# A blocked log-sum-exp over heads: three heads instead of two on TensorE and ScalarE in the half units of tiles 60 and 61

## The chip, the cores and the metric

The kernel runs on one core of one Trainium2 chip. A time is the device time of one execution in microseconds (us). The time before is the median of three executions. A profile is one further execution, taken with the hardware profiler on.

The engines are TensorE (PE; its weight loads are shown as PEld), VectorE (DVE), ScalarE (ACT), GpSimd (POOL) and SyncE (SP), which issues the transfers.

## What is computed

`x` is 8 x 2048 x 2048 (batch, row, column) in fp32, `bias` is 8 x 256. A row of x is cut into 8 heads of 256 columns. For each row and head the result is the log-sum-exp of 256 biased values, written twice next to each other:

```python
x_heads = x.reshape(B, S, H, Dh).transpose(0, 2, 1, 3)
x_heads = x_heads + bias[None, :, None, :]
x_tiled = np.repeat(x_heads, 2, axis=2)
mx = x_tiled.max(axis=-1, keepdims=True)
lse = mx.squeeze(-1) + np.log(np.exp(x_tiled - mx).sum(axis=-1))
```

The kernel sums exponentials without subtracting the maximum, and at its end judges from the largest and smallest sum whether that was safe. If it was not, everything is computed again in a careful way; with these inputs it isn't.

## The kernel before

**Tiles.** 64 tiles of 256 rows each are worked through in order: 128 partitions, with K = 2 rows to a partition. The input lies in four buffers `xb` of four rows each, so that eight tiles are on the chip at a time. When tile t is done, the load of tile t + 8 is put on SP's queue (`reload`); from tile 42 on tiles are loaded one by one, and from tile 57 on in pieces of one row (a half unit).

**Ways to a sum of exponentials.** For one head of one row there are four:
- TensorE writes the bias into a PSUM bank (`put_bias`: a bf16 product of ones with the bias in three parts, L320) and adds x to it by a product with the identity (`add_x`, L338: two passes, since the data are fp32). ScalarE then takes the exponential from PSUM and sums it in the same instruction (`sum_biased`, L393, with a second small instruction that reads the sum).
- ScalarE takes the exponential of x without the bias (`exp_inplace`, L418), and VectorE multiplies it by exp(bias) and sums (`weigh`, L453, one instruction a head and a small one that reads the sum). The factors exp(bias) lie in `one_ps` for heads 1 and 2, `w_ps` for heads 3 to 6 and `w_sb` for 6 and 7.
- The same exponential, but GpSimd multiplies and folds the 256 columns to 32 by halving (`fold`, L469 and L477), and VectorE sums the 32 (`add_fold`, L483).
- In the bulk, GpSimd adds the bias beforehand (L412), and VectorE sums seven heads with one instruction (L437).

**Stages.** A table `STAGES` says from which tile on which mode holds. A mode gives `pe`, the number of heads that TensorE biases; `acc`, those that ScalarE sums; `g0`, from which head on GpSimd adds the bias (8: none); and `fold`, how many heads GpSimd folds. Tiles 0 to 53 are `BULK`, 54 to 56 `MIXED`. From tile 57 on each row of a tile has its own mode: `PROMPT_F1` (two heads on TensorE and ScalarE, five weighed, one folded) in 57 to 61, `SINGLE_F1` (one, six, one) in 62, and in 63 first `PROMPT_F2` (two, four, two) and then `TRIPLE` (three, five, none).

**Order.** The order on each engine is that in which the program issues instructions; it is written out by hand, and the framework adds the waits. A half unit of tiles 57 to 62 issues:
1. `add_x` for this unit's heads on TensorE;
2. `put_bias` for the next unit, then `keep_warm`: three products of the identity with itself into a spare bank, for nothing but activity;
3. what the units before left for later in `for_pool`: VectorE's sum of a folded head, and reloads;
4. `exp_inplace` on ScalarE for all heads that TensorE doesn't have, in one instruction; `fold` on GpSimd;
5. what the unit before left in `for_pe`: its `sum_biased` on ScalarE;
6. `weigh` on VectorE.

The unit's own `sum_biased` is then put into `for_pe`. So on ScalarE the sums of a unit come behind the exponential of the next one.

**PSUM.** Four banks of 512 columns (`ps`, in two tiles called `pair`) take the biased heads of these units in turn. A row with two heads fills one bank. A row with three heads takes one bank for heads 0 and 1 and another, with 256 columns, for head 2.

**End.** After the last sum TensorE transposes the sums of the last batch, ScalarE takes the logarithm, SP stores it; VectorE and TensorE form the verdict, and all engines branch on it.

Of the kernel before, what the change touches and what calls it, by code (L numbers as in the profile page):

```python
# [34 lines left out]
MIXED = dict(pe=1, acc=1, g0=4, late=False, fold=0)  # L35
PROMPT_F1 = dict(pe=2, acc=2, g0=8, late=False, fold=1)
PROMPT_F2 = dict(pe=2, acc=2, g0=8, late=False, fold=2)
SINGLE_F1 = dict(pe=1, acc=1, g0=8, late=False, fold=1)
TRIPLE = dict(pe=3, acc=3, g0=8, late=False, fold=0)
FOLD = 32  # L40
# [8 lines left out]
    (0, (BULK,)),  # L49
    (54, (MIXED,)),  # L50
    (57, (PROMPT_F1, PROMPT_F1)),
    (62, (SINGLE_F1, SINGLE_F1)),
    (63, (PROMPT_F2, TRIPLE)),
]
# [8 lines left out]
def kernel(  # L63
# [9 lines left out]
    H, Dh = bias.shape  # L73
# [8 lines left out]
    MM = 512  # L82
# [42 lines left out]
    def modes_of(t):  # L125
        return [modes for t0, modes in STAGES if t0 <= t][-1]

    def pieces(t):

        if len(modes_of(t)) == 1:  # L130
            return [(0, K, 0, D)]
        cols = [[(0, D)]] * K if t < T - 1 else LAST_COLS
        return [(k, k + 1, c0, c1) for k in range(K) for c0, c1 in cols[k]]
# [59 lines left out]
    def reload(t):  # L193

        n = t + NBUF
        if n < BLOCKS:
            if n % TB == TB - 1:
                load(n - TB + 1)
        elif n < T:
            load(n)  # L200
# [65 lines left out]
    def first_factors():  # L266
        spread(one_ps, V0, W0)
        nc.scalar.activation(out=one_ps, in_=one_ps, func=ACT.Exp)

    def other_factors():  # L270
        nc.scalar.activation(
            out=w_ps[:, W_LATE - W0 :], in_=b_rep[:, W_LATE - G0 : W2 - G0], func=ACT.Exp
        )
        nc.scalar.activation(out=w_sb, in_=b_rep[:, W1 - G0 :], func=ACT.Exp)
# [56 lines left out]
    def add_x(m, t, k0, c0, c1, got):  # L331


        heads = []
        for ka, kb, c, w, bank, p in got:
            if not c0 <= c < c1:
                continue
            mm = nc.tensor.matmul(  # L338
                p,
                lhsT=ident,  # L340
                rhs=xts[t % NBUF][:, ka:kb, c : c + w],
                start=False,
                stop=True,
            )
            on_bank(bank, on_x(t, mm, [loads[t, k0, c0]]))
            for i in range(0, (kb - ka) * w, Dh):
                k, cw = divmod(i, w)
                heads.append((ka + k, (c + cw) // Dh, bank, p[:, i : i + Dh], mm))
        return heads

    def keep_warm():
        for _ in range(NWARM):
            nc.tensor.matmul(  # L353
                tp[:, 0], lhsT=ident, rhs=ident, start=True, stop=True
            )

    def late_heads(m, t, got, sums):


        mms = []  # L360
        for h, p in enumerate(got[:-1]):
            mm = nc.tensor.matmul(  # L362
                p,
                lhsT=ident,
                rhs=xts[t % NBUF][:, :, h * Dh : (h + 1) * Dh],
                start=False,
                stop=True,
            )
            mms.append(on_x(t, mm, [loads[t, 0, 0]]))

        def pe_part():
            for k in range(K):
                act = nc.scalar.activation(  # L373
                    out=xts[t % NBUF][:, k, 0:Dh],
                    in_=got[0][:, k * Dh : (k + 1) * Dh],
                    func=ACT.Exp,
                    accum_out=sums[:, k, 0:1],
                )
                last_uses[t].append(on_x(t, act, [mms[0]]))
            act = nc.scalar.activation(  # L380
                out=xts[t % NBUF][:, :, Dh : m["pe"] * Dh].rearrange(
                    "p k (h j) -> p h k j", j=Dh
                ),
                in_=got[-1].rearrange("p (h k j) -> p h k j", k=K, j=Dh),
                func=ACT.Exp,
            )
            on_x(t, act, [mms[-1]])

        return pe_part

    def sum_biased(t, k, h, bank, p, mm, sums):

        act = nc.scalar.activation(  # L393
            out=xts[t % NBUF][:, k, h * Dh : (h + 1) * Dh],
            in_=p,
            func=ACT.Exp,
            accum_out=sums[:, k, h : h + 1],
        )
        last_uses[t].append(on_bank(bank, on_x(t, act, [mm])))
# [9 lines left out]
    def g_add(m, t, k0, k1):  # L409
        c = m["g0"] * Dh  # L410
        v = xts[t % NBUF][:, k0:k1, c:D]
        add = nc.gpsimd.tensor_tensor(  # L412
            out=v, in0=v, in1=each_row(b_rep, c - G0, D - c, k1 - k0), op=ALU.add
        )
        return on_x(t, add, [loads[t, k0, 0]])

    def exp_inplace(t, v, after):
        return on_x(t, nc.scalar.activation(out=v, in_=v, func=ACT.Exp), [after])  # L418
# [90 lines left out]
    def store():  # L509

        nc.sync.dma_start(
            out=out[0 : B - 1].rearrange("b h (n r) -> (h n) b r", n=NB),
            in_=res.rearrange("q b p k r -> q b (p k r)"),
        )
# [104 lines left out]
    def sums_of(t):  # L619

        b, blk = divmod(t, NBLK)
        if b < B - 1:
            return R[b][:, blk % TB * K :, :, blk // TB]
        return R_last[:, :, blk, :].rearrange("p h k -> p k h")
# [4 lines left out]
    for_pe = []  # L629
# [10 lines left out]
    def flush(later_work):  # L640
        for f in later_work:
            f()
        later_work.clear()

    for t in range(T):
        if t == T_FACTORS:
            other_factors()
        xt = xts[t % NBUF]
        sums = sums_of(t)
        for k0, k1, c0, c1 in pieces(t):  # L650
            m = modes_of(t)[k0]
            add = None
            heads = []
            if c0 == 0:
                bias_here = bias_there
            if m["late"]:
                pe_part = late_heads(m, t, bias_here, sums)
            else:
                heads = add_x(m, t, k0, c0, c1, bias_here)

                def pe_part(t=t, heads=heads, sums=sums):
                    for k, h, bank, p, mm in heads:
                        sum_biased(t, k, h, bank, p, mm, sums)

            if c0 == 0:
                if next_units and not m["late"]:
                    bias_there = put_bias(*next_units.pop(0))
                if t > T_PROMPT and m["g0"] == H:
                    keep_warm()
                if m["g0"] < H:  # L670
                    add = g_add(m, t, k0, k1)
                if t < T - 1 or k0 == 0:
                    flush(for_pool)
            if t == T_PROMPT and (k0, c0) == (0, 0):
                first_factors()
            h0 = max(c0 // Dh, m["pe"])
            h1 = min(c1 // Dh, m["g0"])
            hf = max(h0, min(h1, H - m["fold"]))
            if h0 < h1 and not m["late"]:
                done = exp_inplace(  # L680
                    t, xt[:, k0:k1, h0 * Dh : h1 * Dh], loads[t, k0, c0]
                )
                if hf < h1:
                    for_pool.append(fold(t, k0, hf, h1, sums, done))
            if c0 == 0:
                flush(for_pe)
            if not m["late"]:
                for k in range(k0, k1):
                    for h in range(h0, hf):
                        weigh(  # L690
                            t,
                            xt[:, k, h * Dh : (h + 1) * Dh],
                            h,
                            sums[:, k, h : h + 1],
                            done,
                        )

            def pool_part(t=t, m=m, k0=k0, k1=k1, sums=sums, add=add):
                if add:
                    later(m, t, k0, k1, sums, add)  # L700
                if k1 == K:
                    reload(t)

            for_pool.append(pool_part)
            if m["g0"] < H:
                pe_part()
                if m["late"]:
                    bias_there = put_bias(*next_units.pop(0))
            elif heads:
                for_pe.append(pe_part)  # L710

        fb, at = divmod(t - 2, NBLK)
        if fb >= 0 and at == NBLK - 1:
            finish(fb)
            ends_of(fb)
            if fb == B - 2:
                store()
# [39 lines left out]
```

## Time and profile before

| | |
|---|---|
| median of 3 executions | 326.43 us (326.16 to 326.53) |
| the profiled execution | 327.41 us |
| its span, first to last instruction | 325.5 us |
| mean granted TensorE clock | 0.909 |
| PE busy | 272.7 us (84%) |
| DVE busy | 289.4 us (89%) |
| ACT busy | 265.6 us (82%) |
| POOL busy | 287.5 us (88%) |
| DMA | 135.44 MB, mean 416 GB/s |
| load of one row of a tile (1024 KB), issue to landing | 21.3 us |

The profile counts an engine as busy while an instruction of it runs; a busy TensorE is not TensorE at its peak, since its instructions are pipelined. Neighbouring instructions of ScalarE and VectorE overlap a little in the records, so the step from one start to the next is shorter than a duration. Three views are used: the chain that ended last, followed back from the last instruction, with its shares by engine and by line; windows, which give each engine's busy time in stretches of the span; and the timeline, where a line has the start in us, the duration in us, the engine, the line, the operation, and what is written and read. `xN` counts instructions merged into one line, and a bracket gives idle time before it and what ended it.

### The profile page before, as it was taken

Reading aid. Unit: us, or ns where it says so; the run is one execution under the profiler, and the core shown is the slowest. Engines: PE = TensorE matmul, PEld = TensorE weight load, DVE = VectorE, ACT = ScalarE, POOL = GpSimd, SP = SyncE. Lnnn points to the kernel's source line nnn. Section 1 sums busy time; section 2 is a strip of 40 time slices with the busy share of each in tenths; the row PEclk is TensorE's granted clock in tenths of the full one; section 3 lists DMA queues with packets and bytes.
Section 4 is the critical chain, followed back from the end, with each engine's and each line's share of the span. In section 5 each row is a group of like instructions: output and inputs, shape, how many; then the busy total and the mean of one; then the engine's idle time right before and its main releaser. Section 6 shows DMA issues by size and latency. Waiting matters only on the chain.

```text
span 325.5 us, 2458 instructions
## 1 busy us (share of the span) xinstructions
PE 272.7 (84%) x695; PEld 102.8 (32%) x695; DVE 289.4 (89%) x329; ACT 265.6 (82%) x426; POOL 287.5 (88%) x120
## 2 busy tenths in 40 slices
PE   5999999878898869888688878698999786598983
PEld 2333333322233323332233323233333232135451
DVE  1346879999999998989989999969999999999996
ACT  1157789898598987889889979869899699989993
POOL 6939997999999899999999999999999999858872
PEclk9977899999597997979899979778999799589999
DMA  8999999999999999999999999999999999999992
GB/s 307 464 403 439 451 417 420 447 439 407 443 443 408 437 435 431 423 439 432 419 443 434 415 443 431 407 433 427 427 421 430 429 424 424 417 421 415 421 391 93
DMA packets 8832, 135.44 MB, mean 416 GB/s; under 512 B 1041, under 2 KB 1425, under 8 KB 2417
## 3 DMA queue, kind: packets, MB, share of 16 engines
q1 hardware_dynamic: 8720, 135.27, 98.0%
q8 instruction: 5, 0.08, 0.1%
q14 instruction: 9, 0.07, 0.1%
q10 hardware_dynamic: 98, 0.01, 0.0%
HBM read 134.23 MB, written 1.05 MB: 416 GB/s over the span
## 4 chain that ended last, share of the span: by engine, by line
DVE 43%; DMA 26%; PE 18%; ACT 8%; POOL 3%; issue 0%; SPq 0%; DVEq 0%
DVE R L437 28%; DMA xb<-in_x_dram 26%; DVE xb L453 9%; PE pair L362 7%; ACT xb L418 6%; DVE xb L430 4%; PE one_ps L362 4%; POOL xb L412 3%; PE pair L303 3%; PE one_ps L303 2%; PE pair L235 1%; ACT xb L380 1%; ACT xb L373 1%; DMA brow<-in_bias_dram 1%; ACT res L507 1%
## 5 line engine op out<-in xcount | busy, mean ns | idle before, releaser
L412 POOL TENSOR_TENSOR xb<-xb,b_rep 128x2048 f32<-128x2048 f32 x57 | 257.3, 4537 | 21.3 <-DMA xb<-in_x_dram 21.1
L437 DVE TENSOR_REDUCE R<-xb 128x14 f32<-128x3584 f32 (+1 forms) x57 | 216.8, 3804 | 1.9
L418 ACT ACTIVATE xb<-xb 128x2560 f32<-128x2560 f32 (+5 forms) x77 | 157.5, 2055 | 8.2 <-POOL xb L412 8.0
L362 PE MATMUL pair<-xb,ident 128*128 128x512 f32 x216 | 117.3, 671 | 0.0
L362 PE MATMUL one_ps<-xb,ident 128*128 128x512 f32 x108 | 68.1, 716 | 10.9 <-DMA xb<-in_x_dram 10.9
L380 ACT ACTIVATE xb<-pair 128x1024 f32<-128x1024 f32 x54 | 56.0, 1038 | 25.0 <-PE pair L362 25.0
L362 PEld LDWEIGHTS pair<-xb,ident 128*128 128x128 f32 x216 | 47.0, 218 | 62.6 <-issue 62.6
L430 DVE TENSOR_TENSOR xb<-xb,w_ps 128x512 f32<-128x512 f32 x54 | 36.8, 681 | 24.0 <-ACT xb L418 23.9
L373 ACT ACTIVATE xb<-one_ps 128x256 f32<-128x256 f32 x108 | 40.4, 387 | 6.7 <-PE one_ps L362 6.7
L303 PEld LDWEIGHTS <-ones 3*128 3x128 bf16 (+1 forms) x192 | 16.8, 95 | 78.0 <-issue 69.0
L303 PE MATMUL one_ps<-b,ones 3*128 3x512 bf16 x49 | 19.1, 390 | 20.9 <-ACT xb L373 20.9
L303 PE MATMUL pair<-b,ones 3*128 3x512 bf16 x98 | 29.1, 376 | 0.0
L362 PEld LDWEIGHTS one_ps<-xb,ident 128*128 128x128 f32 x108 | 17.2, 201 | 33.7 <-DMA xb<-in_x_dram 17.3
L338 PE MATMUL pair<-xb,ident 128*128 128x512 f32 (+1 forms) x36 | 20.5, 656 | 6.3 <-DMA xb<-in_x_dram 6.3
L373 ACT ACTIVATION_READ_ACCUMULATOR xb<-one_ps 128x1 f32 x108 | 23.0, 213 | 0.0
L453 DVE CUSTOM_DVE_ANT_0 xb<-xb,w_ps 128x256 f32<-128x256 f32 x61 | 22.3, 416 | 0.0
L477 POOL TENSOR_TENSOR xb<-xb 128x128 f32<-128x128 f32 (+3 forms) x39 | 13.9, 357 | 3.1
L469 POOL TENSOR_TENSOR xb<-xb,w_sb 128x256 f32<-128x256 f32 (+1 forms) x13 | 10.0, 772 | 5.2 <-ACT xb L418 4.6
L353 PE MATMUL tp<-ident 128*128 128x128 f32 x84 | 13.0, 291 | 0.9 <-ACT res L507 0.9
L507 ACT ACTIVATE res<-tp 32x1024 f32<-32x1024 f32 x7 | 7.1, 1011 | 6.2 <-PE tp L497 6.2
L393 ACT ACTIVATE xb<-pair 128x256 f32<-128x256 f32 x33 | 12.0, 368 | 0.0
L353 PEld LDWEIGHTS tp<-ident 128*128 128x128 f32 x84 | 10.5, 191 | 4.3 <-issue 2.8
(55 smaller groups left out, 91.8 us busy)
## 6 DMA issues: line engine op xcount, KB each, us to landing
xb<-in_x_dram SPq DMA_DIRECT2D x20, 4096.0 KB, 21.3
xb<-in_x_dram SPq DMA_DIRECT2D x17, 2048.0 KB, 22.0
xb<-in_x_dram SPq DMA_DIRECT2D x12, 1024.0 KB, 21.3
xb<-in_x_dram SPq DMA_DIRECT2D x4, 256.0 KB, 13.3
out_dram<-res SPq DMA_DIRECT2D x1, 896.0 KB, 6.8
xb<-in_x_dram SPq DMA_DIRECT2D x2, 384.0 KB, 15.9
xb<-in_x_dram SPq DMA_DIRECT2D x2, 128.0 KB, 6.4
out_dram<-res_last SPq DMA_DIRECT2D x1, 128.0 KB, 1.7
```

The lines of the kernel that those rows point to most:

```text
L303: nc.tensor.matmul(p, lhsT=lhsT, rhs=each_row(b, h * Dh, Dh, K), start=i == 0, stop=False,)
L338: mm = nc.tensor.matmul(p, lhsT=ident, rhs=xts[t % NBUF][:, ka:kb, c : c + w], start=False, stop=True,)
L353: nc.tensor.matmul(tp[:, 0], lhsT=ident, rhs=ident, start=True, stop=True)
L362: mm = nc.tensor.matmul(p, lhsT=ident, rhs=xts[t % NBUF][:, :, h * Dh : (h + 1) * Dh], start=False, stop=True,)
L373: act = nc.scalar.activation(out=xts[t % NBUF][:, k, 0:Dh], in_=got[0][:, k * Dh : (k + 1) * Dh], func=ACT.Exp, accum_out=sums[:, k, 0:1],)
L380: act = nc.scalar.activation(out=xts[t % NBUF][:, :, Dh : m["pe"] * Dh].rearrange("p k (h j) -> p h k j", j=Dh), in_=got[-1].rearrange("p ...
L412: add = nc.gpsimd.tensor_tensor(out=v, in0=v, in1=each_row(b_rep, c - G0, D - c, k1 - k0), op=ALU.add)
L418: return on_x(t, nc.scalar.activation(out=v, in_=v, func=ACT.Exp), [after])
L430: mul = nc.vector.tensor_tensor(out=f, in0=f, in1=each_row(w_ps, m["pe"] * Dh - W0, n, k1 - k0), op=ALU.mult,)
L437: red = nc.vector.tensor_reduce(out=sums[:, k0:k1, h0:H], in_=v.rearrange("p k (h j) -> p k h j", j=Dh), op=ALU.add, axis=mybir.AxisListTy ...
L453: ttr = nc.vector.tensor_tensor_reduce(out=v, in0=v, in1=w, scale=1.0, scalar=0.0, op0=ALU.mult, op1=ALU.add, accum_out=dst,)
L477: done = nc.gpsimd.tensor_tensor(out=v[:, :, 0:n], in0=v[:, :, 0:n], in1=v[:, :, n : 2 * n], op=ALU.add)
```

## The change

A new mode `TRIPLE_F1` has three heads on TensorE and ScalarE, four weighed and one folded. Both rows of tiles 60 and 61 take it in place of `PROMPT_F1`. Two lines in the loop change the order: where a unit has more than one bank of biased columns, what stands in `for_pe` is issued before the next unit's `put_bias`; and a `TRIPLE_F1` unit issues its own sums right behind its exponential, and leaves none for the next unit. The first of these lines applies also to the bulk tiles, where `for_pe` is empty, and to the second row of tile 63, where no `put_bias` is left and the order on each engine stays as it was.

```diff
+TRIPLE_F1 = dict(pe=3, acc=3, g0=8, late=False, fold=1)
...
     (57, (PROMPT_F1, PROMPT_F1)),
+    (60, (TRIPLE_F1, TRIPLE_F1)),
     (62, (SINGLE_F1, SINGLE_F1)),
...
             if c0 == 0:
+                if m["pe"] * Dh > MM:
+                    flush(for_pe)
                 if next_units and not m["late"]:
                     bias_there = put_bias(*next_units.pop(0))
...
             elif heads:
                 for_pe.append(pe_part)
+                if m is TRIPLE_F1:
+                    flush(for_pe)
```

In the two programs' lists of instructions this gives, for the four half units together: on VectorE four weighs fewer; on ScalarE four sums more and the four exponentials over 1280 columns in place of 1536; on TensorE four bias products and four x products of 256 columns more. The lists of GpSimd and SP are the same. On ScalarE the sums of the second row of tile 59 stand ahead of the exponential of 60's first row, and the sums of each of the four half units right behind its own exponential.

## The prediction

> **What bounds the kernel now.** I read the chain of waits first, then the busy windows of the last 35 us, then the timeline of that stretch. The chain says which engine the end hangs on:
>
> ```profile
> DVE 43%; DMA 26%; PE 18%; ACT 8%; POOL 3%; issue 0%; SPq 0%; DVEq 0%
> DVE R L437 28%; DMA xb<-in_x_dram 26%; DVE xb L453 9%; PE pair L362 7%; ACT xb L418 6%; DVE xb L430 4%; PE one_ps L362 4%; POOL xb L412 3%; PE pair L303 3%; PE one_ps L303 2%; PE pair L235 1%; ACT xb L380 1%; ACT xb L373 1%; DMA brow<-in_bias_dram 1%; ACT res L507 1%
> ```
>
> The chain in order of time is VectorE alone from 232.65 us to the last sum, at 321.42 us. So VectorE's time, weighs (L453) among it, is the end's time. The windows (us; busy PE, PEld, DVE, ACT, POOL; granted TensorE clock; DMA share; GB/s) say who else has room:
>
> ```profile
> 280.00:285.00 5.00, 2.64 (x5) 0.63 (x4) 5.00 (x14) 4.56 (x7) 4.56 (x2) 0.50 1.01 419
> ...
> 302.00:304.00 2.00, 2.00 (x10) 1.13 (x9) 2.00 (x12) 2.00 (x6) 1.67 (x5) 1.00 1.03 426
> 304.00:306.00 2.00, 1.82 (x9) 1.05 (x9) 2.00 (x14) 2.00 (x6) 1.68 (x5) 1.00 1.01 418
> ...
> 310.00:312.00 2.00, 1.72 (x10) 1.13 (x9) 2.00 (x14) 2.00 (x6) 1.60 (x4) 1.00 0.96 383
> ```
>
> VectorE is full, but ScalarE is full beside it: 2.00 of 2.00 from 290 to 312 us. The change gives ScalarE work, so what decides is how far ScalarE runs ahead. That is in the timeline (start, duration, engine, line):
>
> ```profile
> 302.04 1.47 ACT L418 ACTIVATE xb<-xb 128x1536 f32<-128x1536 f32 x1
> ...
> 303.41 0.36 ACT L393 ACTIVATE xb<-pair 128x256 f32<-128x256 f32 x1
> ...
> 303.77 0.36 ACT L393 ACTIVATE xb<-pair 128x256 f32<-128x256 f32 x1
> ...
> 304.13 1.47 ACT L418 ACTIVATE xb<-xb 128x1536 f32<-128x1536 f32 x1
> ...
> 306.63 0.41 DVE L453 CUSTOM_DVE_ANT_0 xb<-xb,one_ps 128x256 f32<-128x256 f32 x1
> ...
> 308.44 0.41 DVE L453 CUSTOM_DVE_ANT_0 xb<-xb,one_ps 128x256 f32<-128x256 f32 x1
> ...
> 310.39 1.68 ACT L418 ACTIVATE xb<-xb 128x1792 f32<-128x1792 f32 x1
> ```
> ```profile
> 312.15 0.73 POOL L469 TENSOR_TENSOR xb<-xb,w_sb 128x256 f32<-128x256 f32 x1 [0.31 <-ACT xb L418]
> ...
> 312.85 1.70 ACT L418 ACTIVATE xb<-xb 128x1792 f32<-128x1792 f32 x1
> ...
> 313.83 0.41 DVE L453 CUSTOM_DVE_ANT_0 xb<-xb,one_ps 128x256 f32<-128x256 f32 x1
> ```
>
> Seven-head exponentials (1792 columns) belong to tile 62, so the four 1536-wide ones that start at 302.04, 304.13, 306.21 and 308.30 are those of 60/0, 60/1, 61/0 and 61/1 (tile/row). Each of VectorE's half units begins with head 2, read with one_ps: 306.63 (60/0), 308.44, 310.24, 312.04 (61/1), 313.83 (62/0). The exponential of 60/0 ends at 303.51, 3.12 us before VectorE takes it up; that of 62/0 ends at 312.07, 1.76 us before; that of 62/1 at 314.55, 1.43 before its first weigh at 315.98. This lead is all that the change can spend.
>
> **VectorE: four weighs go.** Weigh to weigh is 0.343 us (306.63 to 308.44 is 1.81: five weighs and the reduce of a folded head, 0.10). A half unit of 60 and 61 falls to 1.47, four of them to 5.87 from 306.63: VectorE would stand before 62/0 at 312.50 in place of 313.83 (the four removed are 1.37 us; 0.04 is rounding and the reduce).
>
> **ScalarE: four sums come, 1024 columns go, and one pair moves.** The exponential shrinks from 1536 to 1280 columns, a form that this trace lacks. From 1536 (1.47) to 1792 (1.69) it is 0.22 for 256 columns, from 768 (0.84) to 1536 it is 0.21; I take 1.26, bounds 1.25 and 1.26. The third sum reads another bank and has its own wait on TensorE; tile 63's second row already has such a third sum, 0.36 after the second (starts 318.70, 319.05, 319.41), like the step between the two sums above (303.41 to 303.77). I take 0.355; if the separate wait cost the overlap of 0.09 that neighbouring rows have, it would be 0.45. So a half unit takes 2.09 - 0.21 + 0.355 = 2.23 us in place of 2.09. Sums used to follow the next unit's exponential; now they follow their own, and the pair of 59/1 (0.71) goes ahead of 60/0's exponential. From 302.04: 0.71 + 4 x 2.23 = 9.63, so the exponential of 62/0 starts at 311.67, not 310.39: 1.28 late. Of that, 0.71 comes back at once, since no sums stand between it and 62/1's, and 0.15 more because that one waited for its transfer before; 62/1 starts at 313.26, 0.41 late.
>
> **The new wait.** 62/0's exponential ends at 311.67 + 1.68 = 313.35; ScalarE to GpSimd took 0.08 (312.07 to 312.15), I take that for VectorE too: 313.43. VectorE is there at 312.50 and waits 0.93 us, with everything to the end of the program queued behind. It begins 62/0 at 313.43 in place of 313.83: **0.40 us is left of 1.37**. After that VectorE binds again: 62/1's exponential is done at 314.96, VectorE asks at 315.48. GpSimd's fold of 62/0 starts with VectorE and takes 1.99 (312.15 to 314.14), so its end, 315.42, and hand-over, 315.50, tie with VectorE's reduce (313.43 + six weighs, 2.05 = 315.48): 0.02 lost. Its last fold (3.02 long) would end at 320.4, before VectorE needs it (320.8). ScalarE's last sum ends at 320.3, VectorE's at 321.04. The tail after it, 4.1 us of transpose, verdict and store, stays.
>
> **TensorE.** Per half unit it gets a 256-wide bias product (0.10: the pair of 512 and 256 took 0.42 in place of 0.32 before tile 63's second row) and two 256-column passes (0.43, half of the 0.86 that 512 columns take): 2.04 becomes 2.57. That is slower than ScalarE's 2.23, but TensorE leads: its x products would start at 300.9, 303.8, 306.4 and 308.9, and the first sum of 61/1 is asked for at 310.60 with its bank done at 309.95. So 0.65 us is spare at the tightest. Two banks a unit of four mean that the bias products now wait for the sums of the unit before last: the second of 60/1 waits up to 0.3 us for 59/1's sums (to 302.9; it is in the starts above), and the x products and TensorE's filler matmuls queue behind it; the others come after their sums by 0.2 us or more. Clock: granted 1.00 throughout 290 to 322 us, 0.50 only where TensorE was busy 2.64 of 5.00.
>
> The Trainium skill, TensorE: Matmul & The Clock Gate, section "A second HAM failure mode: psum-queue depth-cycling", speaks against the change: a TensorE that cycles through PSUM banks and idles a little between groups can fall back to half clock and have to warm up again. By the rule the time would be the second rival's below, 328.0; by the window rows above (full clock, with TensorE 91 to 100% busy from 302 to 306 us, and the change adds to that) it is the forecast, 326.05. I go by the rows.
>
> **Queues and transfers.** GpSimd's and SP's lists of instructions stay the same. Tiles 60 and 61 release no load (a tile reloads the one eight later, and 63 is the last), so no transfer moves.
>
> **Sum.** 0.40 - 0.02 = 0.38 off the end. The profiled execution took 327.41 us with a span of 325.5 (1.91 around it): 327.03. It is 0.98 above the median of the runs shown; I take the same difference from that: 326.43 - 0.38 = **326.05 us**. With the dear third sum (0.09 x 4) the gain is 0.02; with a hand-over of nothing 0.46. The likeliest's own range is 325.9 to 326.45.
>
> **Rivals.**
> - All of the 1.37 arrives: 325.06. ScalarE's lead would have to be about 0.95 us larger in the runs without a profile, where 62/0's exponential could start no earlier than its transfer lands (about 310.2). Against it: ScalarE shows no idle time from 290 to 312 us. For it: lead and lag of the two chains were set apart as early as 232 us and may shift by tenths. A half of it, 325.6, is likelier than the whole.
> - TensorE drops to half clock in tile 60 or 61, and the sums, which now stand right in front of the next exponential, make ScalarE wait. Price: a 512-wide product took 2.08 us at 282.90, at clock 0.50, against 1.02; a half unit becomes 5.1 in place of 2.57, 2.5 more, less the 0.65 spare: 1.9 us for one unit, so 328.0. It decides from 0.65 us of delay. Before, the sums stood a unit behind and could not do this.
> - ScalarE's lead is smaller without the profile. The break-even is 0.38 us less lead. If VectorE were 1.35 us earlier, it would already wait for 62/1's exponential before the change (314.63), while the changed kernel still weighs 62/1 from 315.60 (313.43 + 2.05 + 0.02 + the reduce, 0.10): 0.97 us lost, 327.4. Slower by over 0.2% needs 1.03 of that 1.35. For it: the profiled execution is 0.98 longer than the median, and nothing says where.
>
> **How the numbers follow.** 0.2% is 0.65 us, about what a measurement of this kernel can tell from no change. Forecast 0.54 (within 0.2%); part or all of the full gain beyond 0.65 us 0.27 (faster); half clock 0.10 and smaller lead 0.09 (slower by over 0.2%). The range leaves out the whole 1.37 and the far end of the two losses: 325.4 to 326.95.
>
> **What would show it.** VectorE idle by about 0.9 us before 62/0's first weigh, released by ScalarE's L418; four weighs fewer there; ScalarE without idle from 302 to 314; 62/0's exponential 1.3 us later; clock 1.00; TensorE's x products 2.5 to 2.9 apart. It would be wrong if ScalarE idled on TensorE, if VectorE had no gap, or if VectorE waited again in tile 63.

## The result and the profile after

The changed kernel takes 327.14 us (median of 19 executions, 326.76 to 327.57), the kernel before 326.16 us in the same number (325.80 to 327.77): 0.98 us longer, ratio 1.0028 with a 95% interval of 1.0020 to 1.0036. The prediction was 326.05 us in a range of 325.4 to 326.95. The profiled execution after took 326.76 us with a span of 324.9. The profiled execution before took 327.41 us and was an uncommon one: of the 100 executions of that kernel timed beside the changed kernel and the experiments three took as long, 88 lay below 327.0, and the median is 326.09.

The chain that ended last, by engine and by line, on the page of the changed kernel:

```profile
DMA 33%; PE 18%; ACT 18%; DVE 16%; POOL 14%; issue 0%; SPq 0%; DVEq 0%
DMA xb<-in_x_dram 32%; POOL xb L414 14%; ACT xb L420 11%; DVE R L439 11%; PE pair L364 7%; PE one_ps L364 4%; PE pair L305 3%; ACT xb L395 3%; DVE xb L455 2%; DVE xb L432 2%; PE one_ps L305 2%; ACT res L509 2%; PE pair L237 1%; ACT xb L382 1%; ACT xb L375 1%; PE tp L499 1%
```

VectorE held 43% of this chain before and holds 16% now. The same chain in order of time (start, length, what; L420 is the exponential, L395 the sums, L455 the weigh) shows who took over:

```profile
299.90 1.37 ACT xb L420
301.28 1.43 ACT xb L395 x8
302.70 1.16 ACT xb L420
303.86 1.07 ACT xb L395 x6
...
310.56 1.07 ACT xb L395 x6
311.63 1.60 ACT xb L420
313.22 0.02 issue
313.25 0.42 DVE xb L455
```

From 287 to 313 us the end hangs on ScalarE without a break: two pairs of sums in a row (1.43) where one stood before, then four times an exponential of 1.16 and three sums of 1.07, then 62's first exponential, and only behind it VectorE. In the timeline of the changed kernel (start, duration, engine, line):

```profile
302.61 1.25 ACT L420 ACTIVATE xb<-xb 128x1280 f32<-128x1280 f32 x1
...
302.91 0.41 DVE L455 CUSTOM_DVE_ANT_0 xb<-xb,one_ps 128x256 f32<-128x256 f32 x1
...
308.20 0.19 DVE L485 TENSOR_REDUCE R<-xb 128x1 f32<-128x32 f32 x1 [0.59 <-POOL xb L479]
...
310.44 0.19 DVE L485 TENSOR_REDUCE R<-xb 128x1 f32<-128x32 f32 x1 [0.62 <-POOL xb L479]
...
311.53 3.27 ACT L420 ACTIVATE xb<-xb 128x1792 f32<-128x1792 f32 x2
...
312.67 0.19 DVE L485 TENSOR_REDUCE R<-xb 128x1 f32<-128x32 f32 x1 [0.62 <-POOL xb L479]
...
313.25 0.42 DVE L455 CUSTOM_DVE_ANT_0 xb<-xb,one_ps 128x256 f32<-128x256 f32 x1 [0.39 <-ACT xb L420]
```

VectorE now stands idle four times, 2.2 us in all, and the last time it waits for ScalarE. The three waits for GpSimd lead back to ScalarE too: each of the folds waited for began right behind an exponential (at 306.17, 308.40 and 310.63), after GpSimd had stood idle 0.23 to 0.24 us for it. The most telling line is the second: 302.91 is the first weigh of 59/1 (tile/row), a unit that the change doesn't touch. In the profile before the same weigh is this one:

```profile
304.83 0.41 DVE L453 CUSTOM_DVE_ANT_0 xb<-xb,one_ps 128x256 f32<-128x256 f32 x1
```

The exponential that it needs began at nearly the same time in both (299.95 before, 299.81 after). So VectorE was 1.9 us further on already before the change could act. The windows (us; busy PE, PEld, DVE, ACT, POOL; granted clock; DMA share; GB/s) say that ScalarE had no gap and TensorE its full clock:

```profile
302.00:304.00 2.00, 1.94 (x11) 1.08 (x10) 2.00 (x14) 2.00 (x6) 1.18 (x5) 1.00 1.01 418
...
310.00:312.00 2.00, 2.00 (x13) 1.16 (x11) 1.56 (x9) 2.00 (x8) 1.53 (x5) 1.00 0.97 386
312.00:314.00 2.00, 2.00 (x12) 1.36 (x12) 0.98 (x8) 2.00 (x2) 1.26 (x3) 1.00 1.03 393
```

Where did VectorE's 1.9 us come from? From a stage a hundred microseconds earlier. A window and the timeline of the profile before:

```profile
209.00:215.00 6.00, 5.88 (x8) 2.03 (x9) 5.96 (x3) 3.04 (x6) 5.86 (x2) 0.50 1.01 429
```
```profile
209.12 2.07 PE L362 MATMUL one_ps<-xb,ident 128*128 128x512 f32 x2 [1.19 <-DMA xb<-in_x_dram]
...
214.64 1.02 ACT L380 ACTIVATE xb<-pair 128x1024 f32<-128x1024 f32 x1 [2.57 <-PE pair L362]
215.56 2.33 ACT L418 ACTIVATE xb<-xb 128x2560 f32<-128x2560 f32 x1
...
217.92 0.69 DVE L430 TENSOR_TENSOR xb<-xb,w_ps 128x512 f32<-128x512 f32 x1 [2.42 <-ACT xb L418]
```

and of the changed kernel, whose program is the same there:

```profile
209.00:215.00 6.00, 6.00 (x15) 2.32 (x15) 5.97 (x3) 4.86 (x7) 5.97 (x2) 1.00 1.02 434
```
```profile
209.00 1.12 PE L364 MATMUL one_ps<-xb,ident 128*128 128x512 f32 x2 [1.20 <-DMA xb<-in_x_dram]
...
213.60 2.34 ACT L420 ACTIVATE xb<-xb 128x2560 f32<-128x2560 f32 x1 [0.70 <-POOL xb L414]
...
215.97 0.69 DVE L432 TENSOR_TENSOR xb<-xb,w_ps 128x512 f32<-128x512 f32 x1 [0.41 <-ACT xb L420]
```

From 209 to 215 us the granted clock was 0.50 in the profile before and 1.00 in the one after. The products took 2.07 in place of 1.12, ScalarE waited 2.57 for them in place of 0.44, its exponential came 1.96 us later, and VectorE waited 2.42 in place of 0.41. Until then VectorE was at the same place in both (the seven-head reduce ahead of it began at 211.62 and 211.68). It needs 4.5 us a bulk tile, as long as GpSimd that feeds it, and is busy nearly without a gap, so it doesn't make such a delay good: its last seven-head reduce began at 278.92 in the one and at 276.99 in the other.

### The profile page after: what moved, and what is told of

It is laid out like the page before. It is cut to its first block, busy times and chain, and to the rows that moved or that the text cites. A ratio compares the mean times of both kernels' runs of the same rounds, so it can differ in the third digit from the quotient of the medians.

```text
span 324.9 us, 2482 instructions
## 1 busy us (share of the span) xinstructions
PE 275.5 (85%) x707; PEld 105.1 (32%) x707; DVE 288.7 (89%) x321; ACT 265.8 (82%) x434; POOL 287.5 (88%) x120
## 4 chain that ended last, share of the span: by engine, by line
DMA 33%; PE 18%; ACT 18%; DVE 16%; POOL 14%; issue 0%; SPq 0%; DVEq 0%
DMA xb<-in_x_dram 32%; POOL xb L414 14%; ACT xb L420 11%; DVE R L439 11%; PE pair L364 7%; PE one_ps L364 4%; PE pair L305 3%; ACT xb L395 3%; DVE xb L455 2%; DVE xb L432 2%; PE one_ps L305 2%; ACT res L509 2%; PE pair L237 1%; ACT xb L382 1%; ACT xb L375 1%; PE tp L499 1%
## 5 line engine op out<-in xcount | busy, mean ns | idle before, releaser
L420 ACT ACTIVATE xb<-xb 128x2560 f32<-128x2560 f32 (+6 forms) x77 | 156.1, 2038 | 9.3 <-POOL xb L414 9.2
L364 PE MATMUL pair<-xb,ident 128*128 128x512 f32 x216 | 119.2, 681 | 0.0
L364 PE MATMUL one_ps<-xb,ident 128*128 128x512 f32 x108 | 66.6, 702 | 8.9 <-DMA xb<-in_x_dram 8.9
L340 PE MATMUL pair<-xb,ident 128*128 128x512 f32 (+1 forms) x44 | 22.2, 605 | 3.5 <-DMA xb<-in_x_dram 3.5
L455 DVE CUSTOM_DVE_ANT_0 xb<-xb,w_ps 128x256 f32<-128x256 f32 x61 | 22.3, 416 | 0.0
L375 ACT ACTIVATION_READ_ACCUMULATOR xb<-one_ps 128x1 f32 x108 | 22.3, 206 | 0.0
L355 PE MATMUL tp<-ident 128*128 128x128 f32 x84 | 13.7, 301 | 0.6 <-ACT res L509 0.6
L395 ACT ACTIVATE xb<-pair 128x256 f32<-128x256 f32 x37 | 13.3, 364 | 0.0
```

What stands on the lines that cost most here:

```text
L340: mm = nc.tensor.matmul(p, lhsT=ident, rhs=xts[t % NBUF][:, ka:kb, c : c + w], start=False, stop=True,)
L355: nc.tensor.matmul(tp[:, 0], lhsT=ident, rhs=ident, start=True, stop=True)
L364: mm = nc.tensor.matmul(p, lhsT=ident, rhs=xts[t % NBUF][:, :, h * Dh : (h + 1) * Dh], start=False, stop=True,)
L375: act = nc.scalar.activation(out=xts[t % NBUF][:, k, 0:Dh], in_=got[0][:, k * Dh : (k + 1) * Dh], func=ACT.Exp, accum_out=sums[:, k, 0:1],)
L395: act = nc.scalar.activation(out=xts[t % NBUF][:, k, h * Dh : (h + 1) * Dh], in_=p, func=ACT.Exp, accum_out=sums[:, k, h : h + 1],)
L455: ttr = nc.vector.tensor_tensor_reduce(out=v, in0=v, in1=w, scale=1.0, scalar=0.0, op0=ALU.mult, op1=ALU.add, accum_out=dst,)
```

## Experiments

The theory after the result: the profile before showed an execution in which VectorE was late; in most executions it is so early that it has nothing to give, and each delay of ScalarE in tiles 60 and 61 shows. Rivals: the loss lies in the third heads or TensorE's banks themselves, in the moved sums alone, or in the waits for GpSimd's folds. All ratios are to the kernel before on the same chip. They are not ratios of the two medians but lie close to those of the means, and come out up to 0.0007 lower where several executions of the kernel before were long (6 of 35 above 327 us in one set).

One number speaks for the theory across all runs. Up to tile 56 every program here is the same, so the start of VectorE's last seven-head reduce says how late VectorE was in a profile: 278.92 us in the first profile of before, and between 276.59 and 277.61 in the ten others.

**The kernel before once more.** No edit.

> The kernel before, unchanged, profiled once more. Theory (lead): the profiled execution of before, 327.41 us, was one in which TensorE ran at half clock from 209 to 215 us and VectorE started tile 59's second row 3.41 us behind its exponential; without that, VectorE stands about 1.6 us behind it, the last weighs wait for ScalarE, and the time is about 326.2 us, with the last reduce of a fold near 320.0 us in place of 321.19. Rival (the change costs by itself, in TensorE's banks or in the third sums): the lead is again near 3.4 us, VectorE is never idle between 290 and 321 us, and the time is near 327.4 under the profiler.

Measured: 326.12 us (0.9993, 0.9982 to 1.0003); profiled 325.96. Its timeline:

```profile
310.37 1.68 ACT L418 ACTIVATE xb<-xb 128x1792 f32<-128x1792 f32 x1
312.51 0.41 DVE L453 CUSTOM_DVE_ANT_0 xb<-xb,one_ps 128x256 f32<-128x256 f32 x1
312.84 1.70 ACT L418 ACTIVATE xb<-xb 128x1792 f32<-128x1792 f32 x1
...
314.65 0.41 DVE L453 CUSTOM_DVE_ANT_0 xb<-xb,one_ps 128x256 f32<-128x256 f32 x1
```

ScalarE's starts are those of the first profile within 0.02 us (310.39, 312.85). VectorE takes up 62/0 at 312.51 in place of 313.83 and 62/1 at 314.65 in place of 315.98: 1.3 us earlier. The second exponential ends at 314.54, 0.11 us before its first weigh, and the hand-over from ScalarE to VectorE takes 0.04 (313.21 to 313.25 with the change), so ScalarE has 0.07 us to spare there, next to nothing. The last fold's reduce is at 319.86 in place of 321.19. Two details of what was expected were off: VectorE stood 2.1 us behind at 59/1, not 1.6, and it just doesn't wait. A half clock is in this profile too (0.50 from 199 to 205 us), two tiles earlier, with a wait of 2.44 us that ended at 208.36; so it isn't its absence that makes this execution the earlier one.

**The order alone.** Against the changed kernel, the new mode keeps two heads:

```diff
-TRIPLE_F1 = dict(pe=3, acc=3, g0=8, late=False, fold=1)
+TRIPLE_F1 = dict(pe=2, acc=2, g0=8, late=False, fold=1)
...
-                if m["pe"] * Dh > MM:
+                if m is TRIPLE_F1:
                     flush(for_pe)
```

> Two heads as before in tiles 60 and 61, but in the changed kernel's order: 59's last pair of sums ahead of 60's first exponential, each unit's sums right behind its own exponential. Theory (lead): the exponential of 62's first row starts 0.71 us later than before, VectorE waits for it and hands on about 0.3 us: ratio to before 1.001. Rival (the third heads cost, not the order): no change, 1.000. Rival (the order is the whole loss): 1.003.

Measured: 326.59 us against 326.13 (1.0008, 0.9996 to 1.0019). The interval speaks against the order as the whole loss (1.003), but doesn't tell the other two cases apart. In the trace 62's first exponential starts at 311.09 (310.37 in the profile above), VectorE weighs 62/0 from 312.80, and the last reduce is at 320.19: 0.33 us later than 319.86. So moving the sums costs about 0.3 us of the 0.8 that the traces show between before and after (319.86 to 320.64).

**The last sums late.** Against the changed kernel:

```diff
-                if m is TRIPLE_F1:
+                if m is TRIPLE_F1 and (t, k0) != (61, 1):
                     flush(for_pe)
```

> The changed kernel, but the three sums of 61's second row go behind 62's first exponential again. Theory (lead): that exponential starts 1.07 us earlier (310.5 in place of 311.5), 62's second one stays where it is, VectorE starts 62 about 0.4 us earlier and the end comes 0.4 to 0.5 us earlier than in the changed kernel: ratio to before 1.0013 to 1.0017. Rival (ScalarE's order is of no account, TensorE's added work is the loss): as the changed kernel, 1.0028.

Measured: 326.45 us (1.0006, 0.9995 to 1.0017), 0.7 us less than the changed kernel, more than the 0.4 to 0.5 expected. The last reduce is at 320.24, 0.40 earlier than with the change, as expected. The order on ScalarE in front of 62 matters. TensorE's added work is all still there, so it can account at most for what is left: 0.38 us in the traces (319.86 to 320.24), 0.32 in the medians.

**Three heads in tile 60 alone.** Against the changed kernel:

```diff
     (60, (TRIPLE_F1, TRIPLE_F1)),
+    (61, (PROMPT_F1, PROMPT_F1)),
     (62, (SINGLE_F1, SINGLE_F1)),
```

> Three heads in tile 60 alone, 61 as before. ScalarE gets two added sums (0.29 us net) and the moved pair comes back before 62, since 61's first row has no sums waiting. Theory (lead): 62's first exponential starts 0.3 us later than before, about when VectorE gets there, and 62's second one is set by its transfer: ratio 0.999 to 1.001. Rival (each third head costs a quarter of the loss): 1.0014.

Measured: 326.54 us (1.0007, 0.9996 to 1.0018); in the trace the last reduce is at 320.04, 0.18 late. The ratio lies in the theory's range, but the interval holds the rival's 1.0014 as well, so it doesn't tell them apart. VectorE spent what it gained on three waits before 61/0 and 61/1 (1.1 us in all).

**VectorE made late by an added lag.** In both kernels two sums of `b_rep` into a cell that nobody reads stand before tile 57:

```diff
+    idle_sum = sb.tile([P, 1], F32, name="idle_sum")
+
+    def lag(n):
+        nc.vector.tensor_reduce(
+            out=idle_sum, in_=b_rep[:, 0:n], op=ALU.add, axis=mybir.AxisListType.X
+        )
...
     for t in range(T):
+        if t == 57:
+            lag(1024)
+            lag(512)
```

In the kernel before:

> The kernel before, with two idle sums on VectorE (1024 and 512 columns, together about 1.7 us) put before tile 57, into a scratch cell that nobody reads. Theory (lead): VectorE has only about 0.4 us to spare at 62's second row, so the time grows by about 1.3 us: ratio to before 1.004. Rival (VectorE's place is of no account): less than 1.001, or the whole 1.7 us, 1.0052, if VectorE always bounds.

In the changed kernel:

> The changed kernel with the same two idle sums. Theory (lead): its VectorE waits 2.2 us in all in tiles 60 to 62, so the 1.7 us vanish and the time stays that of the changed kernel: ratio to before 1.003, and 0.2 to 0.5 us less than the kernel before with the same lag, so that the change is a gain there. Rival (VectorE bounds, and the change costs in another place): slower by 1.3 us or more again, ratio 1.007.

Measured: the kernel before 327.59 us (1.0043, 1.0025 to 1.0062), the changed kernel 327.02 (1.0026, 1.0012 to 1.0040). The sums took 1.94 us from the first start to the last end and put off what follows by 1.86 (291.71 to 293.57). VectorE stood 0.21 earlier ahead of them than in the second profile of before (277.38 for 277.59), so 1.65 is what they added. The kernel before passed on 1.63 us in the median and in the trace 1.64 (last reduce at 321.50 for 319.86): all of it, since the 0.4 us to spare that was expected weren't there. This run by itself doesn't tell the theory from a VectorE that always bounds (1.0052); the changed kernel's does, since it is where it was without the sums (327.14). Its waits in the profile of that run:

```profile
DVE xb L455 <- ACT xb L420: 0.4, 1, 0.4
DVE R L485 <- POOL xb L479: 0.3, 1, 0.3
```

In the changed kernel's own profile these were 0.4 and, in three waits, 1.8: the late VectorE has used up most of the waits (0.7 us of 2.2 are left), and 62/0 starts at 313.19 (313.25 before). With VectorE late, then, the changed kernel's median is the lower one, by 0.57 us, though the two intervals overlap.

**No fold.** Against the changed kernel, VectorE weighs the eighth head of 60 and 61 itself:

```diff
-TRIPLE_F1 = dict(pe=3, acc=3, g0=8, late=False, fold=1)
+TRIPLE_F1 = dict(pe=3, acc=3, g0=8, late=False, fold=0)
```

> The changed kernel, but in tiles 60 and 61 VectorE weighs the eighth head instead of GpSimd folding it, so its waits for GpSimd there (1.8 us in the changed kernel) are gone and its work is 0.24 us more a half unit. Theory (ScalarE's place decides): VectorE gets to 62's first row by about 312.4 us and still waits for the exponential until 313.25, so the time stays that of the changed kernel: ratio to before 1.0028. Rival (the waits for GpSimd's folds are the loss): faster than the changed kernel by half a microsecond or more, 1.0013 or less.

Measured: 327.08 us (1.0033, 1.0021 to 1.0044), as with the change. In its timeline the waits for GpSimd are gone and one for ScalarE has grown:

```profile
310.63 0.42 DVE L455 CUSTOM_DVE_ANT_0 xb<-xb,w_ps 128x256 f32<-128x256 f32 x1 [0.43 <-ACT xb L420]
...
313.29 0.42 DVE L455 CUSTOM_DVE_ANT_0 xb<-xb,one_ps 128x256 f32<-128x256 f32 x1 [0.85 <-ACT xb L420]
```

62/0 starts at 313.29, with the change at 313.25. The 1.8 us of waiting for folds cost nothing.

**Three heads in one row, nothing moved.** Against the kernel before, with the mode `TRIPLE_F1` and none of the changed order:

```diff
     (57, (PROMPT_F1, PROMPT_F1)),
+    (60, (TRIPLE_F1, PROMPT_F1)),
+    (61, (PROMPT_F1, PROMPT_F1)),
     (62, (SINGLE_F1, SINGLE_F1)),
```

> Three heads in 60's first row alone, and the order of before: no sums are moved. ScalarE gets 0.14 us, VectorE loses one weigh, 0.34 us. Theory (ScalarE's place decides): 62's second exponential is set by its transfer and hardly moves, VectorE now waits 0.3 us for it: ratio 0.9995 to 1.0005, and none of the long runs of before (327.3) since VectorE has something in hand. Rival (every third head costs a quarter of the loss): 1.0007.

Measured: 326.03 us (0.9997, 0.9988 to 1.0006), 325.88 to 326.69 in 11 executions: no difference that can be told. ScalarE's exponential of 62/0 starts at 310.55, 0.18 later than in the second profile of before, that of 62/1 at 312.85, 0.01 later, and VectorE weighs 62/1 from 314.56, right behind its end at 314.52. The wait expected there was spread over 61/0, 61/1 and 62/0 (0.7 us).

**One row and a split exponential.** The same, and 62/1's exponential in two instructions:

```diff
-                done = exp_inplace(
-                    t, xt[:, k0:k1, h0 * Dh : h1 * Dh], loads[t, k0, c0]
-                )
+                cut = 4 if (t, k0) == (62, 1) else h0
+                if cut > h0:
+                    done_low = exp_inplace(
+                        t, xt[:, k0:k1, h0 * Dh : cut * Dh], loads[t, k0, c0]
+                    )
+                done = exp_inplace(
+                    t, xt[:, k0:k1, cut * Dh : h1 * Dh], loads[t, k0, c0]
+                )
```

> As the run with three heads in one row, and the exponential of 62's second row in two instructions (three heads, then four), so that VectorE may begin earlier. Theory: VectorE gains 0.3 us there, but GpSimd's last fold and ScalarE's last sums end at about 319.7 to 320.1 and take over as the bound: ratio 0.9992 to 1.000. Rival (VectorE alone bounds the end): 0.999 or less.

Measured: 326.44 us (1.0010, 1.0001 to 1.0019): a miss, slower than expected. The chain in order of time of its profile:

```profile
313.09 1.69 ACT xb L421 x2
314.78 0.07 issue
314.84 0.74 POOL xb L472
...
316.87 0.18 DVE R L486
317.05 0.33 DVE xb L456
```

The two pieces end at 314.76, later than the one (314.52 in the run above), and with them the head that GpSimd folds; VectorE waits for that fold before tile 63 (0.16 us). GpSimd took over as the bound, earlier than the expectation had it. The split itself explains a part only: the pieces take 1.77 us in place of 1.68, and 0.14 of the delay stands ahead of them, since 62/0's exponential began at 310.69 in place of 310.55. No version beat the kernel before clearly.

## Why the prediction was wrong

**The step that failed** is the transfer from the profile to the median: "It is 0.98 above the median of the runs shown; I take the same difference from that." The difference was not around the kernel but in it: the second profile of before has a span of 324.1 us in place of 325.5 and as much around it (1.86 us, before 1.91), and VectorE's last bulk reduce began at 277.59 in place of 278.92. It was VectorE's lag. With it fell the lead of 1.76 us between 62/0's exponential and its first weigh, which was read correctly from a profile that is not typical. In the second profile of before the lead is 312.51 - 312.05 = 0.46 us, and at 62/1 0.11. The 1.37 us of weighs taken from VectorE then bring nothing, while ScalarE's delay comes through.

**The third rival was the outcome**, with its own sum: VectorE 1.35 us earlier, 0.97 us lost, 327.4 us. Measured: VectorE 1.33 us earlier at 62/1, 0.98 us lost in the medians, 327.14. That 0.97 and 0.98 agree so closely is partly luck: between the traces the loss is 0.78. The rival was given 0.09 and had the strongest evidence in hand, the 0.98 us between profile and median, which the text named for it and then subtracted from the result as if it lay outside.

**ScalarE**, right to the hundredth: 9.63 us from the first moved sum to 62/0's exponential were predicted, and 9.63 are there (301.90 to 311.53). The 1280 columns took 1.25 (1.26 predicted), the third sum stepped by 0.36 with no cost for its own bank. 62/0's first weigh came at 313.25 for 313.43: 0.14 of it because all of ScalarE's stretch began that much earlier in this execution (301.90 for 302.04), and 0.04 because the hand-over to VectorE is 0.04 and not the 0.08 taken from ScalarE to GpSimd. The last reduce came at 320.64 for 320.8. So the changed kernel's course was right; that of the kernel it is measured against was not. Between the traces the loss is 0.78 us (319.86 to 320.64), in the medians 0.98. The 0.2 between comes from the two profiles: that of the changed kernel (326.76) is as fast as the fastest of its 19 executions, 0.38 under their median, the second of before is 0.16 under its own. What makes the other executions of the changed kernel longer is not shown.

**VectorE's wait** was predicted as one of 0.93 us before 62/0, released by ScalarE. There were four: 0.59, 0.62 and 0.62 before 61/0, 61/1 and 62/0 for GpSimd's folds, which the prediction checked only from tile 62 on, and 0.39 for ScalarE. That is a consequence of the same error (VectorE came 1.9 us earlier), and in the run without the fold these waits are gone and nothing is gained.

**TensorE** kept the clock at 1.00 and started its x products at 300.92, 303.72, 306.31 and 308.89 (300.9, 303.8, 306.4, 308.9 predicted). ScalarE did not wait for it. The rule of the Trainium skill that was weighed (TensorE: Matmul & The Clock Gate, section "A second HAM failure mode: psum-queue depth-cycling": cycling through banks can bring the half clock back) didn't show in this stage: the windows above have 1.00. So the second rival did not happen in this execution. The prediction's remark that 0.50 was granted only where TensorE was busy 2.64 of 5.00 holds for the windows it shows, not for the whole trace: from 209 to 215 us it was 0.50 with TensorE busy 5.88 of 6.00. The first rival, all of the 1.37 us, needed a larger lead of ScalarE, and the lead is smaller.

**What stays open:** the change may gain where VectorE is late by chance; the two runs with the added lag point that way (327.02 against 327.59), but their intervals overlap. And the second profile of before is one execution: that the others have a VectorE as early is read from their times and from the ten profiles, not from a trace of each.

## What to carry to other kernels

When the profiled execution stands apart from the median by more than the change is worth, the difference is a term of the sum: find where it lies before any lead or lag is read from that profile, and profile the kernel a second time if that can be had. Where two engines end nearly together, work shifted from one to the other pays only while the first is late; name the lag at which it turns, and ask what sets the lag in the runs that are timed. An order that puts sums ahead of the next exponential is paid by everyone who waits for that exponential: much of the loss came back (0.7 of 0.98 us in the medians, 0.40 of 0.78 in the traces) when three sums went behind one instruction again.

## What was not expected of the hardware

TensorE's half clock in one stage can show at the end, a hundred microseconds later. Six microseconds at a granted clock of 0.50 (209 to 215 us) put VectorE back by 1.9 us against the changed kernel's profile, which had 1.00 there; and since VectorE's bulk pace of 4.5 us a tile equals that of GpSimd in front of it, the delay stood until the end. Where these spells fall differs between executions of one program: 209 to 215 us in the first profile of before, while in the second it was over by 206.

One such spell doesn't make an execution late by itself, since both profiles of before have it, with nearly the same wait of VectorE (2.42 and 2.44 us). Of the 1.33 us between them at the end, 0.53 is there after those two waits (218.64 and 218.11, the same reduce). The other 0.80 comes with two later waits that only the first profile has, of 0.41 us until 223.33 and of 0.20 us until 232.65; ahead of the second of these the granted clock was 0.66 from 225 to 230 us, and 1.00 in the second profile. What sets the place of the spells is not shown.
